# All batches alike, in a ring of three buffers: one change to a masked prefix-sum and matmul kernel

## Chip, core and metric

The kernel runs on one NeuronCore of one Trainium2 chip. The metric is device microseconds of that core. The core has five engines with their own instruction streams: TensorE (PE; PEld is its weight load), VectorE (DVE), ScalarE (ACT), GpSimd (POOL) and SyncE (SP). SP and ACT issue DMAs whose descriptors the hardware makes; POOL issues DMAs whose descriptors software makes, among them the indirect ones, which gather rows by a list of indices. All of them run on the same 16 DMA engines.

## The reference

```python
B, S, D = 8, 8192, 512          # x is [B, S, D] float32, lengths [B], w [D, D]
mask = (pos < lengths[:, None, None])
cs = np.cumsum(x * mask, axis=1)
mid_features = cs[b_idx, lengths // 2, :]
return mid_features @ w          # [B, D]
```

For each batch only the sum of rows 0 to length//2 of x is needed. For the lengths drawn here, 1138, 5379, 511, 4113, 1809, 7542, 7716 and 1140, some 30 MB of x have to be read.

## The kernel before

**Units and chunks.** The rows of x are cut into units of eight rows (16 KB). Which units are needed depends on the lengths, so the kernel works out a list of unit numbers on the chip and gathers 128 units at a time, one to a partition; 128 units are a chunk (2 MB). TensorE adds a chunk up with eight matmuls, one for each row of the units, with a weight matrix of 128 x 8 (partition by batch) that holds a 1 where a row belongs to a batch's sum. The eight matmuls go to four column groups of the array, so their sums stand in four bands of the PSUM bank `s_ps`.

**What is loaded without an index.** Rows 0 to 255 of every batch are loaded first, as two chunks of four batches ("front", L520, issued by SP). Rows 256 to 511 of batches 0 and 1 are loaded last (`xb`, L282), with w behind them in four DMAs (L284 to L288), all issued by POOL. Since batches 0 and 1 have that extra part, `least`, `extra`, `jump` and `shift` hold constants that differ by batch.

**The ring.** `xt` has four buffers. The fronts lie in buffers 0 and 1; POOL gathers the first two chunks into buffers 2 and 3 as soon as VectorE has the list (`idx`). After that, each gather waits until TensorE is done with the buffer's earlier chunk (`s_done`), copies its column of the list to `now` (L269) and issues the gather (L245). The last chunk has a buffer of its own (`xl`), zeroed beforehand by ScalarE (L188), and is gathered in two halves of four rows. ScalarE copies each chunk's weights from `wc` to the ring's weights `wr` (L207). SP waits for weights and data of a chunk and lets TensorE go on (`s_rdy`, L174). Between two chunks TensorE runs two matmuls that nobody reads (`idle`, L449). With these lengths there are 1520 units, so 12 chunks: 11 through the ring (the last two buffers' first turn and nine more) and `xl`.

**Order of the lists.** VectorE works through one stream with a wait before nearly every instruction: the first row (`row`: starts and jumps of the batches), which TensorE broadcasts to all partitions with a matmul by ones (L441); the table `ge`, `z`, `idx` for all 31 possible chunks; a second row (`row2`: half lengths and ends), broadcast by a second matmul; the fronts' weights; and then all 31 chunks' weights in two large instructions, `early` and `wc`.

**The tail.** TensorE's `pe_end` (L472 on) adds `xl`, then for each half of `xb` eight matmuls of 128 columns into `c_ps`; the sums in `s_ps` are turned and folded with four matmuls into `mf_ps` (L495), two of them while the second half of `xb` is awaited; `c_ps` is copied by VectorE and added with one matmul (L498). VectorE copies `mf_ps`, 16 matmuls multiply by w into `o_ps` (L429), VectorE and ScalarE copy the result out, and SP and ACT store a half each. In the program of TensorE, `pe_end` stands ahead of the loop, with a pad of waits behind it (`PAD`), and the start jumps over both.

## Time and profile before

| | |
|---|---|
| median of three runs | 82.9 us (82.73 to 82.91) |
| the profiled execution: its own time | 83.03 us |
| its span, first to last instruction | 81.2 us |
| mean granted TensorE clock | 0.99 |
| moved by DMA | 31.25 MB, 385 GB/s over the span |
| busy: PE, DVE, ACT, POOL | 57.8, 14.1, 8.1, 20.6 us |
| instructions: PE and PEld together, DVE, ACT, POOL | 716, 58, 16, 44 |
| a gather through `now`, from issue to landing | 16.0 us |

The span starts with the program's first instruction, so 1.8 us of the time lie around it. Rows of the timeline give start and duration in us, engine, line, operation and tile, and in brackets what ended the engine's idle time before. A "q" behind an engine's name means its sequencer, which waits, branches and issues. Every fp32 matmul is two MATMUL and two LDWEIGHTS records.

### The profile page before, as it was taken

How to read it: one execution, taken by the hardware profiler on the slowest of the kernel's cores; microseconds unless marked ns; L12 is line 12 of the kernel's file. 1: busy time of each engine (PE TensorE's matmuls, PEld its weight loads, DVE VectorE, ACT ScalarE, POOL GpSimd, SP SyncE). 2: the span in 40 equal slices, each digit the busy share in tenths (PEclk: the TensorE clock that was granted, in tenths of full speed). 3: DMA queues.
4: the chain of work that ended last, by engine and by line, in shares of the span. 5: the costliest groups of instructions: out<-in, count | busy, mean ns of one | idle time of the engine just before them, and what ended most of it. 6: DMA issues, size and time to landing. Idle time of an engine off the chain costs nothing. (4 is left out here: it accounts for less than half of the span.)

```text
span 81.2 us, 1123 instructions
## 1 busy us (share of the span) xinstructions
PE 57.8 (71%) x358; PEld 15.3 (19%) x358; DVE 14.1 (17%) x58; ACT 8.1 (10%) x16; POOL 20.6 (25%) x44
## 2 busy tenths in 40 slices
PE   1962399999939769395894939759396793848840
PEld 1462111112102011020211202011020211104620
DVE  4738899600000000000000000000000000004220
ACT  2991000310100101000010100100000000000020
POOL 4400642515050410505023050379910000000000
PEclk9999999999999999999999999999999999999995
DMA  0999999999999999999999999999999999999500
GB/s 0 307 444 395 428 460 379 387 452 440 395 452 444 396 452 440 395 452 444 395 452 444 395 436 460 396 428 468 395 420 460 404 408 412 416 404 410 220 2 6
DMA packets 2805, 31.25 MB, mean 385 GB/s; under 512 B 386, under 2 KB 402, under 8 KB 914
## 3 DMA queue, kind: packets, MB, share of 16 engines
q0 software_dynamic: 2480, 27.00, 78.9%
q1 hardware_dynamic: 304, 4.20, 12.7%
q8 instruction: 1, 0.02, 0.1%
q10 hardware_dynamic: 18, 0.01, 0.0%
q14 instruction: 2, 0.02, 0.0%
HBM read 31.46 MB, written 0.02 MB: 388 GB/s over the span
## 5 line engine op out<-in xcount | busy, mean ns | idle before, releaser
L429 PE MATMUL s_ps<-xt,wr 128*8 128x512 f32 x208 | 26.4, 628 | 14.3 <-PEq L458 14.2
L449 PE MATMUL idle_ps<-rank,v_f 128*4 128x512 f32 x48 | 23.5, 611 | 0.0
L429 PEld LDWEIGHTS s_ps<-xt,wr 128*8 128x8 f32 x208 | 5.0, 90 | 34.2 <-issue 34.2
L245 POOL DMA_INDIRECT xt<-in_x_dram,now x9 | 9.2, 1021 | 8.0 <-POOLq L271 8.0
L301 DVE COPY s_sb<-s_ps 128x256 f32<-128x256 f32 x2 | 0.8, 424 | 57.3 <-PE s_ps L429 57.2
L269 POOL COPY now<-idx 128x1 int32 x9 | 2.1, 234 | 22.9 <-PE s_ps L429 22.9
L449 PEld LDWEIGHTS idle_ps<-rank,v_f 128*4 128x4 f32 x48 | 4.3, 89 | 17.6 <-issue 17.6
L207 ACT COPY wr<-wc 128x64 f32 x9 | 2.2, 244 | 33.3 <-PE s_ps L429 33.1
L245 POOL DMA_INDIRECT xt<-in_x_dram,idx x2 | 2.2, 1120 | 5.8 <-DVE at_f L301 5.5
L188 ACT ACTIVATE xl<-xl 128x4096 uint32<-128x4096 uint32 x1 | 3.6, 3617 | 0.0
L437 PE MATMUL s_ps<-zero 1*128 1x512 f32 x2 | 2.1, 1135 | 1.8 <-DVE jump L301 1.8
L216 ACT COPY o_sb<-o_ps 8x128 f32<-8x128 f32 x2 | 0.5, 257 | 26.7 <-PE o_ps L429 26.7
L429 PE MATMUL s_ps<-xl,wl 128*8 128x512 f32 x16 | 2.1, 594 | 1.3 <-DMA xl<-in_x_dram,idx_h 1.3
L441 PE MATMUL b_ps<-row,ones 1*128 1x16 f32 x2 | 0.6, 380 | 2.3 <-DVE row L301 2.3
L301 DVE TENSOR_TENSOR wc<-early,ge 128x1984 f32<-128x1984 f32 x1 | 2.2, 2226 | 0.0
L301 DVE TENSOR_TENSOR early<-v,b_ps 128x1984 f32<-128x1984 f32 x1 | 2.2, 2220 | 0.0
L245 POOL DMA_INDIRECT xl<-in_x_dram,idx_h x2 | 2.0, 991 | 0.6 <-issue 0.6
L429 PE MATMUL c_ps<-xb,wb 128*2 128x128 f32 x32 | 1.3, 277 | 0.3 <-DMA xb<-in_x_dram 0.2
L188 ACT ACT_TABLE_LOAD x1 | 1.3, 1283 | 1.5 <-SPq L56 1.5
L429 PE MATMUL o_ps<-wt,mf_sb 128*8 128x128 f32 x32 | 1.2, 273 | 0.3 <-DVE mf_sb L301 0.3
L495 PE MATMUL mf_ps<-fold,s_sb 128*128 128x8 f32 x8 | 1.3, 265 | 0.0
L495 PEld LDWEIGHTS mf_ps<-fold,s_sb 128*128 128x128 f32 x8 | 1.1, 193 | 0.5 <-issue 0.5
(75 smaller groups left out, 23.7 us busy)
## 6 DMA issues: line engine op xcount, KB each, us to landing
xt<-in_x_dram SPq DMA_DIRECT2D x2, 2048.0 KB, 11.2
xb<-in_x_dram POOLq DMA_DIRECT2D x2, 512.0 KB, 18.4
wt<-in_w_dram POOLq DMA_DIRECT2D x1, 512.0 KB, 19.5
wt<-in_w_dram POOLq DMA_DIRECT2D x1, 256.0 KB, 19.6
wt<-in_w_dram POOLq DMA_DIRECT2D x2, 128.0 KB, 19.3
xt<-in_x_dram,now POOLq DMA_INDIRECT x9, 16.0
xt<-in_x_dram,idx POOLq DMA_INDIRECT x2, 12.4
xl<-in_x_dram,idx_h POOLq DMA_INDIRECT x2, 17.3
```

The lines of the kernel that those rows point to most:

```text
L188: act.memzero(xl[:]).then_inc(s_zero, 1)
L207: act.copy(out=weights_of(s), in_=wc[:, bass.ds(col + (R - FRONT - 1), 1)].rearrange("p c e -> p (c e)"),).then_inc(s_wr, 1)
L216: act.copy(out=o_sb[64 * g:64 * g + B, P:], in_=o_ps[64 * g + 32:64 * g + 32 + B, :P],).then_inc(s_act, 1)
L245: pool.indirect_dma_start(out=to, out_offset=None, in_=units, in_offset=bass.IndirectOffsetOnAxis(ap=at, axis=0), bounds_check=n - 1, oob_ ...
L269: pool.tensor_copy(out=now[:, s:s + 1], in_=idx[:, bass.ds(col + (R - FRONT - 1), 1)],).then_inc(s_now, 1)
L301: do(*args, **kw).then_inc(s_dve, 1)
L429: return pe.matmul(to[32 * j:32 * j + weights.shape[1], :rows.shape[1]], lhsT=weights, rhs=rows, start=False, stop=False, skip_group_check ...
L437: pe.matmul(to[:, :width], lhsT=zero[:, :P], rhs=zero[:, :width], start=True, stop=False, skip_group_check=True)
L441: pe.matmul(to[:, :of.shape[1]], lhsT=ones[:], rhs=of[:], start=True, stop=True,).then_inc(s_pe, 1)
L449: pe.matmul(idle_ps[:FB], lhsT=v_f[:, 0], rhs=rank[:].to_broadcast((P, D)), start=True, stop=True, skip_group_check=True)
L495: pe.matmul(mf_ps[:, B * k:B * (k + 1)], lhsT=s_sb[:, at], rhs=fold[:], start=False, stop=False, skip_group_check=True)
```

## The change

- No batch has a part of its own. All batches gather from row 256 on, so the constants by batch are gone. With these lengths that makes 1584 units, 13 chunks (the last with 48 units), instead of 1520 units in 12.
- Rows 64 to 255 are the fronts (`FU` = 6 rows a partition; buffers 1 and 2), and rows 0 to 63 of all batches are loaded last (`xb`, two parts of four batches, two rows a partition), still ahead of w. ScalarE zeroes the two unused rows of buffers 1 and 2, and the PSUM banks, which TensorE zeroed before.
- The ring has three buffers. Gather 0 goes to buffer 0, as soon as `now` is there; gathers 1 and 2 wait for the fronts to be summed. There is no `xl`; all 13 chunks go through the ring.
- The half lengths are made by GpSimd and broadcast with the first row; the second row and its matmul are gone.
- VectorE makes the table for the first three chunks first, then the static weights, the first three chunks' weights, the rest of the table, and after both fronts are summed the weights of the other 28 chunks. Both inputs of `early` now lie in SBUF (`ends` was in PSUM).
- ScalarE, and no longer GpSimd, copies the list's column to `now`.
- The tail sums `xb` in eight matmuls of 256 columns into `d_ps`. All of `pe_end`'s folding comes behind both parts of `xb`: for each half of the columns two matmuls by `fold` and one by `fold2`, into a bank of its own with a copy of its own. ScalarE copies `d_ps`.
- TensorE's program holds 60 matmuls instead of 91, in the order of their use and without the pad.

```diff
-    R = 4
+    R = 3
-    HEAD = 256
-    FRONT = 2
-    BACK = slice(HEAD, HEAD + P * BU)
+    TOP, HEAD = 64, 256
+    PARTS = 2
+    FU, BU = FB * (HEAD - TOP) // P, FB * TOP // P
...
     def scalar(act):
-        act.memzero(xl[:]).then_inc(s_zero, 1)
+        act.memzero(xt[:, 1:, FU * D:]).then_inc(s_zero, 1)
+        for bank in (s_ps, d_ps):
+            act.memzero(bank[:]).then_inc(s_zero, 1)
...
         def weigh(s):
-            act.wait_ge(s_done, free)
+            act.wait_ge(s_done, turn)
+            c = act.snap(turn)
+            act.copy(out=now[:, s:s + 1], in_=idx[:, bass.ds(c, 1)]).then_inc(s_now, 1)
+            if s == 0:
+                act.wait_ge(s_dve, marks["w"])
+            act.copy(out=weights_of(s), in_=wc[:, bass.ds(c, 1)].rearrange("p c e -> p (c e)"),
...
+            act.wait_ge(s_pe, 2)
+            for at in (slice(0, P), slice(P, 2 * P)):
+                act.copy(out=d_sb[:, at], in_=d_ps[:, at]).then_inc(s_act, 1)
...
+                got = fetch(xt[:, c], xu, now[:, c:c + 1], B * UB, s_full[c])
+                if c > 0:
+                    got._wait_ge(s_done, c)
...
         def gather(s):
-            pool.wait_ge(s_done, free)
-            pool.tensor_copy(out=now[:, s:s + 1], in_=idx[:, bass.ds(col + (R - FRONT - 1), 1)],
+            fetch(xt[:, s], xu, now[:, s:s + 1], B * UB, s_full[s])._wait_ge(s_now, 1)
+            pool.sem_inc(s_now, -1)
...
         with nc.body("gp_end", valid_engines=[pool.engine]):
-            for h in range(HALF):
-                fetch(xl[:, h], xh, idx_h[:, h:h + 1], B * S // UH, s_last[h])
+            for f in range(PARTS):
+                pool.dma_start(out=xb[:, f], in_=x[FB * f:FB * (f + 1), :TOP].rearrange(
+                    "b (q u) d -> q b (u d)", u=BU)).then_inc(s_back[f], 16)
...
+        table(now[:], 0, R, B + 1)
+        mark("idx")
...
+        weights(0, R)
+        mark("w0")
+        table(idx[:, R:], R, C, B + 2)
+        mark("table")
...
+        dve.wait_ge(s_done, PARTS)
+        weights(R, C)
         mark("w")
...
         with nc.body("pe_end", valid_engines=[pe.engine]):
+            for f in range(PARTS):
+                pe.wait_ge(s_back[f], 16)
+                for u in range(BU):
+                    at = (R * U + f * BU + u) * B
+                    for h in range(2):
+                        mm = add(d_ps, 2 * u + h, ww[:, at:at + B],
+                                 xb[:, f, u * D + h:(u + 1) * D:2])
             mm.then_inc(s_pe, 1)
+            for i in range(2):
+                pe.wait_ge(s_dve, marks[f"s{i}"])
+                for k in (2 * i, 2 * i + 1):
+                    pe.matmul(mf_ps[i][:, B * (k % 2):B * (k % 2 + 1)], lhsT=s_sb[:, QUARTERS[k]], rhs=fold[:],
+                              start=(k % 2 == 0), stop=False, skip_group_check=True)
+                pe.wait_ge(s_act, i + 1)
+                pe.matmul(mf_ps[i][:], lhsT=d_sb[:, i * P:(i + 1) * P],
+                          rhs=fold2[:].rearrange("p h b -> p (h b)"), start=False, stop=True,
...
-        with nc.body("pe_pad", valid_engines=[pe.engine]):
-            for _ in range(PAD):
-                pe.wait_ge(s_dve, 1)
-            pe.br("pe_0")
```

## The prediction

> **What bounds the kernel now.** I read the page's row of DMA by slices first, then its queues, then the table by stretches at the end of the span, and last the timeline of the tail.

> ```profile
> DMA  0999999999999999999999999999999999999500
> ...
> q0 software_dynamic: 2480, 27.00, 78.9%
> q1 hardware_dynamic: 304, 4.20, 12.7%
> q8 instruction: 1, 0.02, 0.1%
> ```

> The DMA engines are full from the second slice to the 37th: every slice reads 9. Nothing between 2.4 us (first packet of the fronts) and 75 us is paid for by a compute engine, so the time is the start, 31.25 MB at the engines' own pace, and what follows the last bytes. How the bytes end shows in the table by stretches (length; PE, PEld, DVE, ACT, POOL busy with counts; clock; DMA share; GB/s):

> ```profile
> 75.60:75.80 0.20, 0.20 (x9) 0.11 (x2) 0.00 (x0) 0.00 (x0) 0.00 (x0) 1.00 1.13 410
> 75.80:76.00 0.20, 0.20 (x3) 0.20 (x3) 0.16 (x1) 0.00 (x0) 0.00 (x0) 1.00 0.82 287
> 76.20:76.40 0.20, 0.20 (x3) 0.20 (x3) 0.00 (x0) 0.00 (x0) 0.00 (x0) 1.00 0.54 205
> 76.60:76.80 0.20, 0.00 (x0) 0.00 (x0) 0.16 (x1) 0.00 (x0) 0.00 (x0) 1.00 0.17 62
> 76.80:77.00 0.20, 0.12 (x5) 0.12 (x9) 0.03 (x1) 0.00 (x0) 0.00 (x0) 1.00 0.06 21
> ```

> The share falls from 1.13 to 0.06 over 1.2 us: the 16 engines carry equal bytes but do not end together. A DMA has landed only when its slowest engine is through, so each landing is that of the last engine. The tail in the timeline:

> ```profile
> 75.12 0.33 PEld L429 LDWEIGHTS c_ps<-xb,wb 128*2 128x2 f32 x16
> 75.69 0.52 PEld L495 LDWEIGHTS mf_ps<-fold,s_sb 128*128 128x128 f32 x4 [0.24 <-issue]
> 75.84 0.29 DVE L301 COPY c_sb<-c_ps 128x128 f32<-128x128 f32 x1 [1.28 <-PE c_ps L429]
> 76.19 0.30 PEld L498 LDWEIGHTS mf_ps<-pick,c_sb 128*128 128x128 f32 x2
> 76.64 0.19 DVE L301 COPY mf_sb<-mf_ps 128x32 f32<-128x32 f32 x1 [0.50 <-PE mf_ps L498]
> 76.88 0.93 PEld L429 LDWEIGHTS o_ps<-wt,mf_sb 128*8 128x8 f32 x32 [0.40 <-DVE mf_sb L301]
> 77.98 0.60 DVE L301 COPY o_sb<-o_ps 8x128 f32<-8x128 f32 x2 [1.15 <-PE o_ps L429]
> ```

> The second half of `xb` lands at 75.08 (the chain of waits ends its 18.7 us DMA piece there) and TensorE goes through the tail without waiting for w; the result's copy starts at 77.98, 2.86 after 75.12.

> **Bytes.** Fronts: 8 x 192 rows instead of 256, 3.15 MB for 4.20. Gathers: 1584 units of 16 KB instead of 1520, 25.95 MB for 24.90. `xb` and w stay at 1.05 MB each. The sum is 31.25 MB both times, and the list deals a part chunk's units out evenly, so each of the 16 engines keeps its sixteenth. In the packet records a 16 KB row takes 0.611 us on its engine and a 4 KB row 0.164; 12 KB must lie near 0.46. So the stream's length is unchanged: cost 0, bounds -0.1 and +0.1.

> **The start.** The first row no longer waits behind constants, the zeroing matmuls are gone, and the table is 27 elements wide for 279, so the first gather can issue near 6 us instead of 8.54. That gains nothing, since the fronts fill the engines until about 10 us (12.5 before). Gathers 1 and 2 are the ones to watch, because they now wait for sums of fronts. TensorE runs three idle matmuls behind the broadcast, two records each at the cold 0.85 us (the idle row at 12.96 shows that pace), until some 8.9; the first front (before: 9.5, now 8 rows x 0.15 us = 1.2 earlier) is there by 8.3; its sum takes 1.9 us warm and 3.6 cold (row at 9.59), so it is done between 10.7 and 12.5. POOL needs 0.8 to issue, 1.0 for the descriptors (rows of 1.02), and I add 1 for the first bytes: gather 1 streams from 13.5 to 15.3. Gather 0 keeps the engines busy until 10 + 8 x 0.61 = 15. So it is covered, or late by 0.3. Gather 2 has a new neighbour: VectorE's `early` and `wc` over 28 chunks start at the very moment that releases it. This row pair bears on it:

> ```profile
> 12.12 2.23 DVE L301 TENSOR_TENSOR wc<-early,ge 128x1984 f32<-128x1984 f32 x1
> 13.73 0.66 POOL L269 COPY now<-idx 128x1 int32 x1 [2.65 <-PE s_ps L429]
> 18.09 0.18 POOL L269 COPY now<-idx 128x1 int32 x1 [1.80 <-PE s_ps L429]
> ```

> POOL's copy took 0.66 us under `wc` and ended with it, against 0.18 with VectorE idle. If the gather's reading of its list is held in the same way, gather 2 (released near 15) starts when `early` ends (28/31 of 2.22, 2.0 us) or when `wc` ends (4.0 us), and streams from 19.3 or 21.3. Gather 1 covers until 20. I take the first: 0, bounds 0 and 1.5.
> [...]

> **The ring of three.** A chunk's landing is followed by 1.9 us of TensorE (the 1.90 row at 15.71), 1.5 until the gather starts (before: sum done near 17.6, gather at 19.15; `now` moves to ScalarE at 0.24 for 0.18 and counts the same), 1.0 of descriptors and my 1.0 for first bytes: 5.5 with 0.1 for SP's relay. Meanwhile two chunks, 9.8 us, stand in the queue, of which landing itself has used about 1.6 (packet records: last engine 1.1 behind, 0.5 to the wait). Cover is 2.7 us: cost 0. If it were short, every third period would pay. Before, three chunks covered it, which the 16.0 us from issue to landing shows.
> TensorE sums 15 chunks for 13 and `xl`, 1.9 each, with 1.7 of idle matmuls, in a period of 4.9: hidden. At the end chunk 13 (48 units, 1.8 us of stream) lands some 2.6 ahead of `xb`; TensorE is through it and the first part of `xb` about 0.2 before the second lands, and VectorE's two copies of `s_ps` (0.42 each) run beside that: hidden, narrowly.

> **The tail, from the second `xb` landing.** Eight matmuls of 256 columns stream as many columns as sixteen of 128: 0.57 (75.69 - 75.12). ScalarE's copy starts at 0.72 as VectorE's did, takes 0.29 (nearest row, c_sb) and 0.06 to TensorE: first `fold2` at 1.07. By then two `fold` matmuls are issued (four loads, 0.11 apart). From there: two loads 0.22, four 0.45, two 0.22; second bank's result 0.34 + copy 0.19 + 0.05 after its second load at 1.85: 2.43. The matmuls by w start at 1.96 and their second half, which began 0.34 after the first before, waits to 2.43; from there to the copy it was 0.76. Sum 3.19 against 2.86: **+0.33 us**. What is lost is cover: before, half of the folding ran while the second `xb` was awaited. Bounds +0.2 (banks overlap better) and +0.6 (ScalarE at the 0.30 that its long copies scale to, no overlap).

> **Sum.** 83.03 + 0.33 = 83.36 for the profiled execution. The median lies 0.13 below that, so 83.2.

> **Rivals.**
> *Late engine freed (faster).* Page part 3 has one instruction packet on q8; in the packet records it is 16 KB at 2.23 us, took 1.38, and the engine that carried it starts its first front row at 3.6 instead of 2.4 to 2.8. It stays about 1 us behind in every gather (last semaphore writes of the first: 18.75, the next 18.40, most by 17.8). [...] If the block isn't loaded then, `xb` lands earlier: by 0.2 if the next engine stays where it is (74.34 against 74.51 in its landing), by up to 1.0 if all end together. It outweighs the tail's 0.33 from there on: 82.2 to 83.0, likeliest 82.5. For it: equal bytes, unequal ends. Against it: other engines are late too (second to fourth by 0.2 to 0.4), and the block may be loaded at another time.
> [...]
> *Starved ring (slower).* Gather 2 behind both large VectorE instructions, or a cold first sum: 1 us, at most 2, that all engines lose: 84.2.
> *Even.* The late engine gains 0.2 to 0.4 and the tail gives it back: 82.9.

> **Chances.** Forecast 0.42, late engine freed 0.28, starved ring 0.17, even 0.13. A measurement of this kernel can tell about 0.2% (0.17 us) from no change. Of the forecast 0.04 falls inside that bound. Faster 0.28, same 0.17, slower 0.55. The range reaches from 82.3 into the freed engine's case to 84.1 in the starved one.

> **What will show it.** The tail from second `xb` to the first result copy: 3.2 us if right. The DMA row must stay at 9 around 15 to 21 us; a 5 there is the starved ring. The q8 line, and the fall of the DMA share at the end: over 1.2 us again if the late engine stays, within 0.5 if freed. Gather to landing near 11 us with slack, near 8 if the ring runs dry. Wrong if `xb`'s second landing moves by more than 0.3 us from 75.1.

## The result and the profile after

The changed kernel takes 82.82 us (median of 6 runs, 82.66 to 82.92), the kernel before 82.91 (median of 6, 82.73 to 84.16): ratio 0.9995, 95% interval 0.998 to 1.001. No difference that can be measured. The profiled execution took 82.92 us with a span of 80.4 us (80.45). Here the two numbers part: the span is 0.75 us shorter than before (81.20), the time only 0.11. In all comparisons below, spans and times are medians of the executions that the ratio uses; those with a fallen clock are left out.

The page of the changed kernel, rows of DMA and queues:

```profile
DMA  0899999999999999999999999999999999999700
...
q0 software_dynamic: 2480, 28.05, 82.4%
q1 hardware_dynamic: 304, 3.15, 9.7%
q8 instruction: 1, 0.02, 0.1%
```

The row stands at 9 through 15 to 21 us (slices 8 to 11), so the ring never ran dry at the start. There is one 16 KB instruction packet on q8, as before. The count does not tell when: in the packet records it is now at 76.05 us (it took 1.10) and no longer at 2.23 (1.38). The two 8 KB packets on q14 that lay inside the run before (18.87 and 31.52 us) are gone from the page; the records have one at 82.73 us, 2.3 us behind the last instruction.

How the bytes end, by stretches of 0.2 us (busy times, clock, DMA share, GB/s):

```profile
75.40:75.60 0.20, 0.20 (x4) 0.20 (x3) 0.00 (x0) 0.00 (x0) 0.00 (x0) 1.00 1.15 410
75.60:75.80 0.20, 0.20 (x4) 0.20 (x3) 0.17 (x1) 0.00 (x0) 0.00 (x0) 1.00 0.67 225
75.80:76.00 0.20, 0.20 (x4) 0.20 (x4) 0.00 (x0) 0.00 (x0) 0.00 (x0) 1.00 0.38 123
76.00:76.20 0.20, 0.20 (x5) 0.17 (x5) 0.00 (x0) 0.00 (x0) 0.00 (x0) 1.00 0.47 123
76.20:76.40 0.20, 0.20 (x9) 0.20 (x12) 0.10 (x1) 0.00 (x0) 0.00 (x0) 1.00 0.01 0
```

The share falls from full to nothing in 0.7 us (the row at 76.00 holds the instruction packet too), where before it took 1.2 and still stood at 0.06. The last data packet ends at 76.27 us instead of 77.20. The chain of waits, in order of time (start, duration), before:

```profile
56.37 18.70 DMA xb<-in_x_dram
75.08 0.04 issue
75.12 0.64 PE c_ps L429 x14
...
77.98 0.28 DVE o_sb L301
```

And after:

```profile
64.33 9.75 DMA xb<-in_x_dram
74.09 0.04 issue
74.13 0.64 PE d_ps L395 x8
74.77 0.57 PE mf_ps L446 x4
75.34 0.23 PE mf_ps L449 x2
75.57 0.46 PE mf_ps L446 x4
76.03 0.23 PE mf_ps L449 x2
76.26 1.00 PE o_ps L395 x32
77.26 0.02 issue
77.28 0.28 DVE o_sb L276
```

The second `xb` has landed at 74.09, 0.99 ahead of before. From the first matmul on it to the result's copy it is 77.28 - 74.13 = 3.15 us, against 2.86. So the last instructions come 0.7 us earlier. And yet the time doesn't: around the span lie 2.47 us instead of 1.83. Three moves, -0.99, +0.29 and +0.64, sum to nearly nothing. The experiments ask where the first and the last of them come from.

A DMA's landing is sixteen semaphore writes in the record (for the second `xb` before, from 73.74 to 75.08 us); I take each to be one engine's share. The records don't name the engines, and which of them held the second `xb` back I read from the times. Before, nine came from 73.74 to 74.03 us and seven from 74.40 on, the last two at 74.85 and 75.08. The last engine is late from the fronts on, behind the packet at 2.23 us (the first front's last write is at 9.44, the next at 8.59). The one at 74.85 turns late in the gather behind the 8 KB packet at 18.87 us (six late writes, 23.45 to 24.11, for five in the gather ahead), the one at 74.40 in that behind the packet at 31.52 (a seventh, at 33.19). The other four lag from the first gather on (18.55 to 18.80, where eleven are in by 18.15), and no run tells why. After the change all sixteen lie within 0.53 us. So without the three that, by their times, carried instructions the landing before would have been at 74.66: of the 0.99 us this accounts for 0.42. The rest goes with the four others, so by these times the fetches are a part of the cause and not all of it. The size varies, too: another trace of the changed kernel (its base run below) has the landing at 74.50.

### The profile page after: what moved, and what is told of

Its sections match the earlier page's. It is cut to its first block, busy times and chain, and to the rows that moved or that the text cites. A ratio compares the mean times of both kernels' runs of the same rounds, so it can differ in the third digit from the quotient of the medians.

```text
span 80.4 us, 1176 instructions
## 1 busy us (share of the span) xinstructions
PE 59.6 (74%) x360; PEld 14.1 (18%) x360; DVE 11.8 (15%) x43; ACT 9.7 (12%) x31; POOL 19.9 (25%) x32
## 2 busy tenths in 40 slices
DMA packets 2803, 31.23 MB, mean 388 GB/s; under 512 B 434, under 2 KB 450, under 8 KB 962
## 3 DMA queue, kind: packets, MB, share of 16 engines
q0 software_dynamic: 2480, 28.05, 82.4%
q1 hardware_dynamic: 304, 3.15, 9.7%
## 4 chain that ended last, share of the span: by engine, by line
issue 59%; POOL 14%; DMA 14%; PE 5%; DVE 2%; POOLq 2%; ACTq 0%; SPq 0%
POOL xt L228 14%; DMA xb<-in_x_dram 12%; DMA lens<-in_lengths_dram 1%; PE mf_ps L446 1%; PE o_ps L395 1%; PE d_ps L395 1%; PE bc_ps L408 1%; DVE o_sb L276 1%; POOL xb L257 1%; POOLq L245 1%; PE mf_ps L449 1%; POOLq L228 0%; DVE row L276 0%; POOLq L126 0%; DVE ge L276 0%
## 5 line engine op out<-in xcount | busy, mean ns | idle before, releaser
L395 PE MATMUL s_ps<-xt,ww 128*8 128x512 f32 x240 | 29.5, 598 | 14.6 <-PEq L415 14.6
L401 PE MATMUL idle_ps<-ones 128*4 128x512 f32 x58 | 29.6, 637 | 0.0
L228 POOL DMA_INDIRECT xt<-in_x_dram,now x13 | 14.8, 1135 | 45.9 <-POOLq L252 36.7
L395 PEld LDWEIGHTS s_ps<-xt,ww 128*8 128x8 f32 x240 | 5.9, 89 | 37.8 <-issue 37.6
L401 PEld LDWEIGHTS idle_ps<-ones 128*4 128x4 f32 x58 | 5.1, 90 | 20.4 <-issue 20.4
L185 ACT COPY now<-idx 128x1 int32 x10 | 1.9, 192 | 44.1 <-PE s_ps L395 44.1
L276 DVE TENSOR_TENSOR early<-v_f,ends 128x192 f32<-128x192 f32 (+1 forms) x2 | 2.4, 1192 | 5.5 <-PE s_ps L395 5.5
L188 ACT COPY ww<-wc 128x64 f32 x10 | 2.4, 244 | 0.1
L276 DVE TENSOR_TENSOR wc<-early,ge 128x192 f32<-128x192 f32 (+1 forms) x2 | 2.4, 1192 | 0.1
L166 ACT ACTIVATE xt<-xt 128x2048 uint32<-128x2048 uint32 x1 | 1.9, 1910 | 0.0
## 6 DMA issues: line engine op xcount, KB each, us to landing
wt<-in_w_dram POOLq DMA_DIRECT2D x1, 256.0 KB, 10.7
xt<-in_x_dram,now POOLq DMA_INDIRECT x13, 11.7
```

The lines of the kernel that those rows point to most:

```text
L166: act.memzero(xt[:, 1:, FU * D:]).then_inc(s_zero, 1)
L185: act.copy(out=now[:, s:s + 1], in_=idx[:, bass.ds(c, 1)]).then_inc(s_now, 1)
L188: act.copy(out=weights_of(s), in_=wc[:, bass.ds(c, 1)].rearrange("p c e -> p (c e)"),).then_inc(s_wr, 1)
L228: return pool.indirect_dma_start(out=to, out_offset=None, in_=units, in_offset=bass.IndirectOffsetOnAxis(ap=at, axis=0), bounds_check=n - ...
L276: do(*args, **kw).then_inc(s_dve, 1)
L395: return pe.matmul(to[32 * j:32 * j + weights.shape[1], :rows.shape[1]], lhsT=weights, rhs=rows, start=start, stop=False, skip_group_check ...
```

## The experiments

**Theory.** One cause for the first and third: the packets that the page calls `instruction`, 16 KB on q8 and 8 KB on q14, which I take for blocks of the engines' programs being fetched. The one at 2.23 us held its DMA engine for 1.38 us among the data, and by the times above that engine was last in each landing up to the second `xb`'s; the theory is that such a fetch in the stream makes the landings late, and that the change shortened the programs and so moved the fetches, TensorE's to the end of the stream, another engine's behind the last instruction. **Rivals.** The fetches don't matter: the fronts' other sizes set the late engine, and the time around the span is the launch's. Or VectorE's large instructions decide: a gather under `early` took 2.65 us, the other twelve 1.0 in the mean.

**TensorE's program laid out as before** (the tail ahead of the loop again, the loop at the same place as before):

```diff
+        with nc.body("pe_end", valid_engines=[pe.engine]):
...
+            pe.br_cmp(begin, 0, "pe_pad", END, "IS_GT")
+        with nc.body("pe_pad", valid_engines=[pe.engine]):
+            for _ in range(176):
+                pe.wait_ge(s_dve, 1)
+            pe.br("pe_0")
```

> The changed kernel with TensorE's program laid out as before: the tail first, a pad, then the loop at the same place in the program as before. Block theory (the 16 KB instruction block at 2.2 us makes one DMA engine 1 us late): the block is back near 2.2 us, the second xb lands near 75.1 us instead of 74.1, the span is 81.4 instead of 80.4. If the time around the span hangs on TensorE's layout too, it falls from 2.5 to 1.8 and the time is 83.2; if not, 83.8. Rival (the ring of three or the smaller fronts made the landing early): landing 74.1, span 80.4, time 82.8.

Measured: ratio to before 1.0187 (1.0113 to 1.0261, from three executions), span 82.0. The block is back at 2.23 us (1.44), and the second `xb` lands at 75.60, 1.5 us later than in the changed kernel. That is more than the engine's lag, and a table by stretches shows why (same columns):

```profile
19.00:20.00 1.00, 1.00 (x12) 0.20 (x8) 0.97 (x2) 0.00 (x0) 1.00 (x1) 1.00 0.67 279
20.00:21.00 1.00, 1.00 (x10) 0.26 (x3) 1.00 (x1) 0.00 (x0) 0.01 (x1) 1.00 1.13 262
21.00:22.00 1.00, 1.00 (x4) 0.17 (x2) 0.20 (x1) 0.06 (x1) 0.00 (x0) 1.00 0.52 164
```

Against 410 GB/s, 131 + 148 + 246 KB are missing, 1.3 us of stream; 98 KB of them had come early, in the row before (508 GB/s at 18 to 19 us), which leaves 1.0. This is the starved ring. The engine that carried the block holds the second front back (its last packet ends at 13.8 us, at 11.8 without the block), its sum starts at 14.47 for 12.33 and meets a clock of 0.50 at 16 to 18 us, and gather 2 is released late and then held:

```profile
17.12 2.03 DVE L276 TENSOR_TENSOR early<-v_f,ends 128x1792 f32<-128x1792 f32 x1 [8.29 <-PE s_ps L395]
17.35 2.66 POOL L228 DMA_INDIRECT xt<-in_x_dram,now  x1 [5.49 <-PE s_ps L395]
```

Its descriptors are done at 20.0 us and the engines wait. In the gap the late engine caught up, so the two losses did not add: the sixteen semaphore writes of a gather lie 1.49 us apart at 21.8 us and 0.56 at 27.1, and the last data ends at 77.77 with the share falling within 0.6 us. What the lag alone costs shows ahead of the gap. Gather 0 has landed at 16.75 us; in the eleven other traces of the changed kernel and its variants, none with a block this early, it has at 15.79 to 16.16. The mean of its sixteen writes, 15.64, lies among theirs (15.42 to 15.70), so it is one engine and not the stream: 0.6 to 1.0 us. The layout matters, and by a longer way than the lag alone. Why the clock fell in that stretch, no run tells.

**The kernel before, with its program in order of use** (`pe_end` behind the loop, no pad, no jump; nothing else):

```diff
-            pe.br_cmp(begin, 0, "pe_pad", END, "IS_GT")
-        with nc.body("pe_pad", valid_engines=[pe.engine]):
...
+            pe.br(END)
...
-    nc.tensor.br_cmp(begin, 0, "pe_end", "pe_0", "IS_GT")
+    nc.tensor.br("pe_0")
```

> The kernel before with TensorE's program in the order of use: no jump over the tail, no pad. Block theory: no block at 2.2 us, the second xb lands near 74.1 instead of 75.1, the span is 80.2 instead of 81.2; the time is 82.0 if the time around the span stays at 1.8, and 82.7 if it grows to 2.5 with the layout. Rival (ring or fronts): landing 75.1, span 81.2, time 82.9.

Measured: 1.0038 (1.0007 to 1.0069), no gain. The block moved from 2.23 to 66.91 us, still inside the stream, and one engine is late again: the second `xb` lands at 75.54, not near 74.1 as the theory had it. The end by stretches:

```profile
75.60:75.80 0.20, 0.20 (x8) 0.19 (x12) 0.00 (x0) 0.00 (x0) 0.00 (x0) 1.00 1.10 410
76.80:77.00 0.20, 0.20 (x2) 0.14 (x2) 0.00 (x0) 0.00 (x0) 0.00 (x0) 1.00 0.11 41
77.40:77.60 0.20, 0.20 (x12) 0.20 (x16) 0.00 (x0) 0.00 (x0) 0.00 (x0) 1.00 0.05 20
```

0.05 is a sixteenth of the engines, nearly: one engine alone is busy until 77.65. Of the sixteen writes of a landing the last stands 0.31 us behind the next in the gather ahead of the block and 0.67 in all that follow, the second `xb` included. So the order in itself gained nothing. The changed kernel's program is in order of use too, with 60 matmuls for 91, and its block came in the tail, at 76.05, 0.2 us ahead of the last data's end. The lags behind the block at 2.23 us and behind the one at 66.91 both last to the second `xb`, 0.23 and 0.67 us; the one late engine that caught up did so in the gap of the run above.

**VectorE's large instructions later**, one chunk after gather 2's release:

```diff
-        dve.wait_ge(s_done, PARTS)
+        dve.wait_ge(s_done, PARTS + 1)
```

> The changed kernel with VectorE's two large weight instructions released one sum later (after the first gathered chunk). Both theories: gather 2 is no longer held, 1.0 us for 2.65. Cover theory (gather 1 still streams until 20 us): second xb within 0.1 us of 74.1, time within 0.2 us of 82.8. Starved-ring theory: 0.5 to 1 us faster. If the weights come too late for the fourth chunk instead, slower by up to 1 us.

Measured: 0.9967 (0.9938 to 0.9996) to before, span 80.6, beside 0.9991 (0.997 to 1.0012) and 80.7 for the changed kernel in the runs after these, on another chip: no difference that can be told. In the trace the second `xb` lands at 74.75, not within 0.1 us of 74.1; but that execution's span, 81.1, is 0.5 above the median. The timeline of the changed kernel, then of this one:

```profile
14.29 2.02 DVE L276 TENSOR_TENSOR early<-v_f,ends 128x1792 f32<-128x1792 f32 x1 [5.46 <-PE s_ps L395]
14.53 2.65 POOL L228 DMA_INDIRECT xt<-in_x_dram,now  x1 [2.91 <-PE s_ps L395]
```

```profile
14.65 0.99 POOL L228 DMA_INDIRECT xt<-in_x_dram,now  x1 [2.43 <-PE s_ps L395]
18.04 2.02 DVE L276 TENSOR_TENSOR early<-v_f,ends 128x1792 f32<-128x1792 f32 x1 [9.22 <-PE s_ps L395]
18.88 2.05 POOL L228 DMA_INDIRECT xt<-in_x_dram,now  x1 [3.24 <-POOLq L252]
```

Gather 2 is free (0.99 instead of 2.65), the next one is held instead (2.05). So a gather is held under `early` (2.65 and 2.05 us, 0.99 without), and that cost nothing that the ratio can tell: the queue covered it (share 0.94 and 1.03 at 14 to 18 us in the changed kernel). In the run above, where the late release had used up the cover, hold and release together left the gap.

**Pads behind the ends of GpSimd and VectorE** (28 and 24 instructions that never run; on record, 54 and 46 waits and a jump each):

```diff
+            pool.br_cmp(gate, 0, "gp_pad", END, "IS_GT")
...
+        dve.br_cmp(gate, 0, "dv_pad", END, "IS_GT")
```

> The changed kernel with 28 and 24 instructions that are never run behind the ends of GpSimd's and VectorE's programs, so that these are as long as before. If the 0.7 us that the time around the span grew by comes from where their last code lies (an 8 KB instruction block is loaded 2.3 us after the span), it falls from 2.5 to 1.8 and the time is 82.2. Rival (it hangs on TensorE's program, or on something else): 2.5 stays, time 82.8.

Measured: 1.0092 (1.0061 to 1.0124), span 81.8; around the span 2.09 us (2.07 to 2.16), and nothing above that. So no execution has 2.5 us around the span any more, but the time is 83.96, not the expected 82.2. Two 8 KB packets appear, at 78.81 and 81.54 us. The first took 0.47 us, and one piece of the first store ended right behind it (79.33 after 79.28), 0.5 us after its other pieces; the second store's last piece came at 79.38, 0.2 after its others. GpSimd, which waits for both stores, went on 0.99 us after that instead of 0.37, and needed 0.49 us from its jump to the next instruction instead of 0.18. Why its wake-up took longer isn't shown. Here blocks at the end hurt too: a store's piece and GpSimd's wait ended behind them.

**Where are the blocks cheap?** In the next runs each engine has its pad in other places: the changed kernel itself once more, then GpSimd's pad ahead of its first gather, VectorE's ahead of its wait for the last chunk, and both:

```diff
+        pool.br_cmp(gate, 0, "gp_pad", "gp_b_0", "IS_GT")
+        with nc.body("gp_pad", valid_engines=[pool.engine]):
+            for _ in range(62):
+                pool.wait_ge(s_dve, 1)
...
+        dve.br_cmp(gate, 0, "dv_pad", "dv_1", "IS_GT")
+        with nc.body("dv_pad", valid_engines=[dve.engine]):
+            for _ in range(50):
+                dve.wait_ge(s_dve, 1)
```

> The changed kernel once more, beside the kernel before on the same chip, as the base of the three runs with pads. Both theories: span 0.7 to 0.9 us under that of before, time around the span 2.1 us in about half the executions and 2.5 in the others, against 1.8 for before; so the time 0.1 to 0.5 us lower than before.

> The changed kernel with 32 instructions that never run put into GpSimd's program ahead of its first gather, so that GpSimd has 102 instructions (before: 100, changed: 69). Theory (what lies around the span grew because 8 KB instruction blocks of GpSimd or VectorE that were loaded at 18.87 and 31.52 us before are loaded after the span's end now): if both blocks were GpSimd's, they are loaded during the run again and the time around the span is 1.8 us, the time 0.3 to 0.7 us under the changed kernel's; if one was, one block of 8 KB shows in the run and the time around the span falls by about half of the 0.3 to 0.7. Rival (it comes from something else, as TensorE's program or the launch): around the span 2.1 to 2.5 us as in the changed kernel.

> The changed kernel with 26 instructions that never run put into VectorE's program ahead of its wait for the last chunk, so that VectorE has 86 instructions (before: 84, changed: 58). Theory (instruction blocks of GpSimd or VectorE): 1.8 us around the span if the blocks were VectorE's, half of the gain if one was, and 2.1 to 2.5 us if both were GpSimd's. Rival (something else): 2.1 to 2.5 us.

> Both pads together, GpSimd 102 and VectorE 86 instructions. Theory: two blocks of 8 KB are loaded in the run, 1.8 us around the span, span 80.5 to 80.8 as in the changed kernel (each load holds one DMA engine for 0.3 us while the run goes on), so the time 82.3 to 82.6 us where before has 82.9. Rival: 2.1 to 2.5 us around the span and the time of the changed kernel, or up to 0.3 us above it.

| kernel | ratio to before | span | around the span | 8 KB packets at |
|---|---|---|---|---|
| before, same chip | | 81.3 | 1.81 (1.76 to 1.87) | |
| changed, again | 0.9991 (0.997 to 1.0012) | 80.7 | 2.45 (2.13 to 2.64) | 83.19 |
| GpSimd's pad | 1.0004 (0.9983 to 1.0024) | 80.9 | 2.15 (2.05 to 2.22) | 23.09 |
| VectorE's pad | 1.0063 (1.0036 to 1.009) | 81.2 | 2.41 (2.03 to 2.55) | 19.97 |
| both | 1.0037 (1.0014 to 1.006) | 81.2 | 2.11 (2.00 to 2.15) | 20.00, 22.56 |

The base repeats the account: -0.6 of span, +0.64 around it, time 83.08 for 83.10. GpSimd's pad takes the packet behind the end away, and with it every execution above 2.3 us; with VectorE's, six of nine still lie above. Over all runs, 29 of 42 executions without a pad of GpSimd's lie above 2.3 us, and none of 76 with one. The traces without that pad agree one by one: the packet is there in the three executions with 2.5 to 2.6 us around the span, and absent in the two with 2.1 (late weights, VectorE's pad). So the block that is fetched behind the last instruction, in some executions, is GpSimd's, and costs some 0.35 us there. Put into the stream it costs 0.2 us of span: that only trades one loss for another. VectorE's pad costs 0.5 us of span, more than its packet's 0.31 on one engine; in its trace the gather behind the packet lands 5.28 us after the one ahead, where the period is 4.90, so 0.4 of the 0.5 is the engine's lag. Neither pad brings 1.8 back, nor do both bring the expected 82.3 to 82.6 us (83.31), so the theory held for half of what lies around the span and not for the rest.

**GpSimd's block in the gap between stream and store**, and then the same with TensorE's or ScalarE's and SyncE's programs lengthened too:

```diff
             pool.dma_start(out=wt[:, 3, at], in_=w[QUARTERS[3], at]).then_inc(s_w[2 + g], 16)
+            gate = pool.alloc_register("gate_gp")
+            pool.reg_mov(gate, 0)
+            pool.wait_ge(s_dve, marks["s1"])
+            pool.br_cmp(gate, 0, "gp_pad", "gp_fin", "IS_GT")
...
+            pe.br_cmp(gate, 0, "pe_pad", END, "IS_GT")
...
+        act.br_cmp(gate, 0, "ac_pad", "ac_0_0", "IS_GT")
...
+        sp.br_cmp(gate, 0, "sy_pad", "sy_0_0", "IS_GT")
```

> The changed kernel with 32 instructions that never run in GpSimd's program behind its last DMA issue and a wait for the second copy of the sums, so that GpSimd's next 8 KB block is asked for near 75 us, when the stream is all but over. Theory (in the run, as with the early pad, a block costs 0.2 to 0.3 us of span because one DMA engine is late by it; behind the span it costs about 0.35): the block is loaded at 75 to 78 us, the span is 80.4 to 80.7 us as in the changed kernel, and around the span lie 2.05 to 2.2 us in every execution; time 0.2 to 0.6 us under before on the same chip. Rival (a block at the end is always in somebody's way): the last store, or GpSimd's wake-up after it, comes 0.3 to 0.5 us later and the time is that of the changed kernel or above it.

> The same, and 151 instructions that never run at the end of TensorE's program (424 instead of 272 instructions; before has 427). Theory A (the 0.3 us by which 2.1 us around the span stands above the 1.8 of before are TensorE's: its program ends 155 instructions earlier): around the span 1.8 us. Theory B (another engine, or not the instruction blocks at all): around the span 2.05 to 2.2 us as without this pad.

> GpSimd's late pad, and 33 instructions that never run in ScalarE's and in SyncE's programs ahead of their rings (93 and 74 instead of 60 and 41). Theory A (the 0.3 us are TensorE's): around the span 2.05 to 2.2 us, and the span up to 0.5 us longer, since up to two blocks of 8 KB are loaded in the run. Theory B (ScalarE's or SyncE's end code): 1.8 us around the span.

| kernel | ratio to before | span | around the span | 8 KB packets at |
|---|---|---|---|---|
| before, same chip | | 81.4 | 1.79 (1.73 to 1.86) | |
| GpSimd's late pad | 0.9935 (0.9906 to 0.9964) | 80.6 | 2.12 (2.00 to 2.19) | 75.90 |
| and TensorE's | 0.9909 (0.9876 to 0.9941) | 80.7 | 2.06 (2.01 to 2.15) | 75.92 |
| and ScalarE's, SyncE's | 0.9964 (0.9938 to 0.999) | 80.8 | 2.15 (2.04 to 2.22) | 27.39, 76.28 |

With the pad late, the page's queues read:

```profile
q8 instruction: 1, 0.02, 0.1%
q10 hardware_dynamic: 18, 0.01, 0.0%
q14 instruction: 1, 0.01, 0.0%
```

The q14 line is back, but now the packet flies beside the q8 one at 76 us, behind nearly all data and ahead of the store (77.6), so it is in nobody's way. 82.68 us for 83.18: this kernel beats the one before by 0.6%. By their ratios to it, it beats the changed one too, whose interval (0.997 to 1.0012) begins just above the end of this one (0.9964); the two were not run side by side. The edit is 32 instructions that never run and one wait with a jump. TensorE's pad adds nothing that its interval can tell, ScalarE's and SyncE's cost span for one more block in the stream. None brings the 1.8 back.

**The three pads together**, GpSimd 103, VectorE 86, TensorE 424 instructions, as the change found them (100, 84, 427):

> The changed kernel with the three pads at once: GpSimd's late one (103 instructions), VectorE's ahead of its wait for the last chunk (86) and TensorE's at the end (424), so that these three programs are about as long as before (100, 84, 427). Theory A (the 0.3 us left around the span are instruction blocks of VectorE and TensorE together, the later of the two deciding, so that neither pad alone showed anything): 1.8 us around the span; with the 0.2 to 0.5 us of span that VectorE's block costs in the run, the time is 82.5 to 82.8 us where before has 83.1. Theory B (not the instruction blocks of these engines): 2.0 to 2.2 us around the span, time 82.7 to 83.2 us.

Measured: 1.0027 (1.0003 to 1.0051), span 81.2, around the span 2.06 us (1.99 to 2.16). Theory A is wrong: with program lengths as before, 0.26 us more than before's 1.80 still lie around the span. All runs of kernels built on the changed one have at least 1.99 there, all those of the two built on before at most 1.87. What makes the 0.3 us stays open; none of the lengths that were tried, alone or three together, takes it away.

## Why the prediction came out as it did

The time, 82.82, lay in the range, but the likeliest case (83.2) did not happen, and the sum that came true is not the one that was written down. Its own sign of being wrong came: the second `xb` moved by 0.99 us, where more than 0.3 was to count against it. That the time fell into the range even so is luck: the gain at the end of the stream and the loss around the span, neither of them in the sum, cancelled.

- **Sum: 83.03 + 0.33.** This is the step that failed. It held the end of the stream where it was and put nothing on what lies around the span. The end came 0.99 us earlier, and around the span came 0.64 more (as much between medians, side by side).
- **Late engine freed.** Rightly named, down to the packet, and the upper bound of its gain, 1.0, was reached in the profiled execution (0.58 in the other trace). Of that, 0.23 is the named engine's, the prediction's lower bound; the rest is engines that it counted against the case, two of which, by their times, carried the 8 KB packets. Its condition was half seen: "if the block isn't loaded then". It is loaded at 76.05, in the tail. That the change would move the block at all no row of before showed; the runs do: TensorE's old layout brought it back to 2.23 us, the straight kernel's order of use alone to 66.91, where an engine was late again, and with the shorter program too it came at 76.05. TensorE is not alone in this: pads of GpSimd's and VectorE's brought 8 KB packets to 23.09 and 19.97. "The block may be loaded at another time" stood there as a reason against, which it was for a place inside the stream (66.91 us) and was not for one behind it.
- **What the fetches cost.** The one at 76 us held nothing up that the chain shows: the matmuls by w around it took 1.00 us, 1.07 before. Those at 2.23 and 66.91 us each left one DMA engine last at the end, 0.23 and 0.67 us behind the next. TensorE's block was of 16 KB in these runs, and GpSimd's and VectorE's were of 8 KB.
- **Even** gave 82.9 and was right in the time, by other terms than its own: it had 0.2 to 0.4 from the engine, less the tail. What evened things out was a third term that no case held.
- **Tail.** +0.33 predicted, +0.29 in the chain, 3.15 us for 3.19. The step was right.
- **Start.** Gather 2 was held and let through between the two large instructions, as taken: `early` ended at 16.31, the gather's descriptors at 17.18, and `wc` went on beside it. It cost nothing (share 0.94 at 14 to 16 us, 1.03 at 16 to 18), and nothing changed when it was freed. The bound of 1.5 was a fair one: 1.0 to 1.3 us were lost where the release came 2.8 us later.
- **The hold itself.** That a gather would be held as the copy was (0.66 us for 0.18) was an estimate, and it came true: 2.65, 2.66 and 2.05 us under `early`, against 0.99 without, each ending 0.86 or 0.87 us after `early` did. In the kernel before, whose `early` took one input from PSUM, a gather under it (10.05 us) took 1.03. Which of the differences between the two makes the hold, no run tells.
- **Ring of three, bytes, TensorE.** Right: 11.7 us from issue to landing (11 taken), 31.23 MB, the DMA row at 9 throughout, and the copies of `s_ps` were through at 74.41, ahead of the matmuls that wait for them (74.70).

## What to carry to other kernels

When DMA binds, look for the engine that ends last and for what it carried besides: here the engine that carried a 16 KB instruction packet ended last in the kernel before, with the packet at 2.23 us, 0.23 us behind the next, and in its straight form, with it at 66.91, 0.67 behind, and two that, by their times, carried 8 KB were late as well. Program length and order were a tuning parameter here: a jump over 32 dead instructions moved GpSimd's packet from 83.19 to 75.90 us, behind nearly all data and ahead of the store, and the kernel ran at 0.9935 of before, where the changed one had 0.9991 on another chip. And compare times beside spans: here the span was 0.75 us shorter and the time 0.11, and an 8 KB packet lay behind the last instruction.
